# First chunk of a two-layer encoder: modulation rows as stationary operands on TensorE in every quarter, turned x copied by ScalarE, lower parts by VectorE

## The chip, the cores and the metric

The kernel runs on 1 core of one Trainium2 chip. The metric is the device time of one execution in microseconds; lower is better. The engines are named as in the profile: PE is TensorE (PEld its load of stationary operands), DVE is VectorE, ACT is ScalarE, POOL is GpSimd, and SP is the engine whose queue issues the DMAs.

## The reference

Two layers over x (512 tokens by 1024, float32). Only the start of a layer matters here:

```python
cs = silu(c)                                   # (1, 1024)
for l in range(2):
    mod = cs @ w_ada[l] + b_ada[l]             # 3072 columns
    shift, scale, gate = split(mod, 3)
    h = rms_norm(x, norm_g[l]) * (1 + scale) + shift
    proj = h @ w_in[l]                         # 3712 columns
    ...                                        # three kinds of heads, each with a gate
    x = x + gate * (concat(oa, ob, oc) @ w_out[l])
```

So `mod` is a product of one row with a 1024x2048 matrix (shift and scale), needed before the first product of h with `w_in`, and it must be summed over 1024 rows of `w_ada`.

## The kernel before

Every big product is made in float32 precision out of three products of parts: a factor is split into an upper part (the copy to `fp32r`, always by ACT) and a lower part (the difference, by DVE or POOL), and `products` (L331 to L333) multiplies upper by upper, upper by lower and lower by upper. hT and hL are the two parts of the turned h, `whi` and `wlo` (in the first chunk `stq`, `stk` and, for the odd quarters, `stB`, `stC`) those of the weights.

The first chunk multiplies h by 768 columns of `w_in` (for the retention heads). It runs over four quarters q of D (256 columns of h each, so also 256 rows of `w_in`), and in each over four tiles of 128 tokens: `first_chunks`, 16 groups of 12 products into PSUM tiles `acc` (512 columns) and `scw` (256 columns). A quarter can start when its piece of the modulation is there. For that the class `Start` loads eight "rows" of w_ada per quarter (row r holds 128 rows of the matrix, one per partition, by 512 columns, 256 of shift and 256 of scale) and sums them weighted by `cs`:

- rows named in `PE_ROWS[q]` are multiplied on PE, with `cs[:, r]` as stationary operand of one column and the row as 512 moving columns, into one PSUM row `line` (L517); before, this is so for six rows of quarter 0 alone;
- of the others ACT makes the first (`act(self.a, w, AF.Copy, scale=v)`), and DVE adds each of the rest to `ada_acc` (L159 by way of `stt`);
- `close` sums `ada_acc` over the partitions by four products with the 128x128 blocks of `ada_acc` as stationary operand and one column of ones (`over_rows`, L510), and turns `line` into columns by way of an SBUF copy `lsb` and four 1x1 products. The result `ada_ps` is read by DVE into `mod`.

```python
        def over_rows(self, w, v, stop=False):
            ps = self.ps.rearrange("p j k -> p (j k)")
            for i in range(4):
                T.matmul(ps[:, i:i + 1], w[:, i * P:(i + 1) * P], v, start=False, stop=stop and i == 3)
```

Meanwhile x is loaded in four token tiles x0 to x3; `norm_x` squares and sums each on ACT (`junk`), takes the root on DVE and POOL (`rstd`) and scales it in two halves (`xn`, the engine of each by a letter of `X_NORM`); `turn_x` transposes 128x128 blocks on PE into PSUM (`xps`, L1210) and copies them out (`xT`, engines by `X_OUT`). `Start.turn` makes hT (ACT), h (DVE) and hL (engines by `H_SUB`: V is DVE, G is POOL). `Wide.split` makes the weights' parts, with the lower part of one half on POOL and of the other on DVE (L375).

The string `START` gives the order in which these steps are written out; from it a scheduler sets the order of the instructions on each engine, and each engine runs its own in that order. The rows of w_ada go through a pool of five buffers of two rows each (`raw`); SP issues a load only when its buffer is free, in the order of the program.

Of the kernel before, what the change touches and what calls it, by code (L numbers as in the profile page):

```python
# [19 lines left out]
P = 128  # L20
# [34 lines left out]
PE_ROWS = (0, 2, 4, 5, 6, 7), (), (), ()  # L55
# [3 lines left out]
X_NORM, X_OUT, H_SUB, LINE = "AGAGVAVV", "AVVVAVVVAVAVAAAV", "VGGVVGVVGV", "AAAAAAAV"  # L59
# [75 lines left out]
def encoder(ctx, tc, x, c, norm_g, w_ada, b_ada, w_in, w_out, params, consts, out):  # L135
# [222 lines left out]
    class Wide:  # L358
# [10 lines left out]
        def split(self):  # L369
            z = [one.tile([P, 3 + (n != "stC"), S], F32R, name=n) for n in (("stq", "stk"), ("stB", "stC"))[self.q % 2]]  # L370
            self.hi, self.lo = (y.rearrange("p a n -> p (a n)")[:, :1536].rearrange("p (k n) -> p k n", k=2) for y in z)
            for j in range(2):
                c_ = slice(j * 384, j * 384 + 384)
                act(self.hi[:, :, c_], self.raw[j])
                (V if j else G).tensor_tensor(self.lo[:, :, c_], self.raw[j], self.hi[:, :, c_].bitcast(F32), OP.subtract)  # L375
# [107 lines left out]
    ENG = {"V": V, "G": G}  # L483

    def copy(e, o, i):
        V.tensor_copy(o, i) if e == "V" else act(o, i)

    class Start:
# [11 lines left out]
        def open(self):  # L500
            q = self.q
            self.ps = ps = pv_p.tile([P, 2, 2], F32, name="ada_ps", tag="pv")
            self.a = self.line = None
# [8 lines left out]
        def row(self, r):  # L512
            w, v = self.raw[r], cs[:, r:r + 1]
            if r in PE_ROWS[self.q]:
                if self.line is None:
                    self.line = acc_p.tile([P, 512], F32, name="line", tag="acc")
                T.matmul(self.line[0:1], v, w, start=r == PE_ROWS[self.q][0], stop=r == PE_ROWS[self.q][-1])  # L517
# [6 lines left out]
        def close(self):  # L524
            q, ps = self.q, self.ps
            if self.a is not None:
                self.over_rows(self.a, ones[:, 0:1], self.line is None)
            if self.line is not None:
                z = one.tile([P, 512], F32, name="lsb", tag="s9")
                for i in range(2):  # L530
                    copy(LINE[2 * q + i], z[0:1, i * 256:i * 256 + 256], self.line[0:1, i * 256:i * 256 + 256])
                self.over_rows(z[0:1], ones[0:1, 0:1], True)
# [4 lines left out]
        def turn(self, ts):  # L537
# [4 lines left out]
            for k in range(2):  # L542
# [5 lines left out]
                ENG[H_SUB[(2 * q + 2 if q else ts[0]) + k]].tensor_tensor(lo, h[:, :n], hi.bitcast(F32), OP.subtract)  # L548
# [643 lines left out]
    def norm_x(t):  # L1192
# [6 lines left out]
        for j in range(2):  # L1199
# [3 lines left out]
            else:  # L1203
                ENG[X_NORM[2 * t + j]].tensor_scalar(*z, rs, None, OP.mult)

    def turn_x(t, q):
# [4 lines left out]
        for k in range(2):  # L1211
            copy(X_OUT[4 * q + t + k], xT[2 * q + k][:, t * P:(t + 2) * P], ps[:, k].rearrange("p t m -> p (t m)"))
# [82 lines left out]
```

## Time and profile before

| | us |
|---|---|
| median of 3 runs (675.12 to 678.33) | 677.21 |
| the profiled execution, its own time | 676.71 |
| its span, first to last instruction | 674.9 |
| PE busy | 630.2 (93%) |
| DVE busy | 501.0 (74%) |
| ACT busy | 330.4 (49%) |
| POOL busy | 261.4 (39%) |

The span is that of the program's own instructions. Busy time is the union of an engine's instructions; PE's matmuls overlap one another, so of PE the distance from one start to the next tells more than a duration. A float32 product is recorded as two passes. Granted clock is the share of TensorE's full 2.4 GHz, of which the profile knows two levels, 0.50 and 1.00.

### The profile page before, as it was taken

What the parts mean: (1) busy time and instruction counts of PE and PEld (TensorE: products, weight loads), DVE (VectorE), ACT (ScalarE), POOL (GpSimd) and SP (SyncE); (2) the same over time, 40 slices, a digit from 0 to 9 for tenths busy, and PEclk for the clock granted to TensorE, in tenths of its full rate; (3) what the DMA queues carried; (4) which work ended last, traced back from release to release, by engine and by line L of the source; (5) the groups of instructions that cost most, each with busy time, mean ns of one, the idle gap of its engine ahead of it and who ended that gap; (6) DMA issues with size and microseconds to landing.
All of it is one profiled execution on the core that took longest, in us unless ns stands there. A gap on an engine that the chain in (4) does not pass through costs nothing.

```text
span 674.9 us, 10503 instructions
## 1 busy us (share of the span) xinstructions
PE 630.2 (93%) x3487; PEld 516.0 (76%) x3487; DVE 501.0 (74%) x1157; ACT 330.4 (49%) x722; POOL 261.4 (39%) x252
## 2 busy tenths in 40 slices
PE   6889998999999996999998999989999999989997
PEld 2778787977887784677776998887778887767786
DVE  1998697589988988897769154768997888576443
ACT  5534352447655674554423243434757476656410
POOL 3427363666343520211457252767052613121200
PEclk9789998999999999899999999999999999999999
DMA  9796133344555556575643122235454625423211
GB/s 316 250 335 159 57 94 97 105 120 120 148 127 173 144 165 170 166 243 181 216 166 119 32 83 75 64 84 155 114 156 119 193 85 161 116 64 133 93 63 63
DMA packets 87134, 93.20 MB, mean 138 GB/s; under 512 B 7044, under 2 KB 68004, under 8 KB 87080
## 3 DMA queue, kind: packets, MB, share of 16 engines
q1 hardware_dynamic: 87080, 92.53, 45.6%
q8 instruction: 28, 0.46, 0.3%
q14 instruction: 26, 0.21, 0.1%
HBM read 72.58 MB, written 4.19 MB: 114 GB/s over the span
## 4 chain that ended last, share of the span: by engine, by line
PE 41%; DVE 8%; POOL 4%; issue 2%; ACT 2%; DMA 0%; POOLq 0%; ACTq 0%; DVEq 0%; SPq 0%
PE acc L333 8%; PE acc L332 8%; PE acc L331 8%; PE tr L554 5%; PE pv L703 3%; PE acc L327 1%; PE acc L329 1%; PE acc L328 1%; DVE wlo L302 1%; PE sc L726 1%; PE sc L787 1%; DVE ada_acc L159 1%; PE sc L788 1%; DVE pt L693 1%; PE ada_ps L464 1%
## 5 line engine op out<-in xcount | busy, mean ns | idle before, releaser
L331 PE MATMUL acc<-whi,hT 128*128 128x384 f32 (+1 forms) x424 | 155.4, 366 | 1.5 <-ACT vc L156 1.0
L333 PE MATMUL acc<-whi,hL 128*128 128x384 f32 (+1 forms) x424 | 153.2, 361 | 0.0
L332 PE MATMUL acc<-wlo,hT 128*128 128x384 f32 (+1 forms) x424 | 152.7, 360 | 0.0
L302 POOL TENSOR_TENSOR wlo<-raw,whi 128x768 fp32r<-128x768 f32 (+1 forms) x26 | 55.1, 2119 | 126.4 <-ACT whi L156 119.2
L156 ACT ACTIVATE whi<-raw 128x768 fp32r<-128x768 f32 (+1 forms) x75 | 69.6, 929 | 52.9 <-PE acc L333 41.6
L331 PEld LDWEIGHTS acc<-whi,hT 128*128 128x128 f32 x424 | 80.2, 189 | 8.5 <-ACT vc L156 1.4
L302 DVE TENSOR_TENSOR wlo<-raw,whi 128x384 fp32r<-128x384 f32 (+1 forms) x98 | 64.1, 683 | 28.6 <-ACT whi L156 28.3
L333 PEld LDWEIGHTS acc<-whi,hL 128*128 128x128 f32 x424 | 80.1, 189 | 6.2
L332 PEld LDWEIGHTS acc<-wlo,hT 128*128 128x128 f32 x424 | 80.2, 189 | 5.7
L159 DVE SCALAR_TENSOR_TENSOR ada_acc<-raw,cs,ada_acc 128x512 f32<-128x512 f32 x86 | 72.3, 845 | 5.3 <-DMA raw<-in_w_ada_dram 2.7
L199 POOL TENSOR_TENSOR qkss<-qkss,nhalf 128x4 f32<-128x4 f32 (+1 forms) x40 | 54.1, 1352 | 49.2 <-DVE qkss L569 48.2
L156 ACT ACTIVATE e<-sc,mx 128x512 f32<-128x512 f32 x64 | 43.9, 688 | 37.7 <-DVE mx L728 23.3
L728 DVE TENSOR_REDUCE mx<-sc 128x1 f32<-128x512 f32 x64 | 43.1, 684 | 9.9 <-PE sc L726 9.6
L156 ACT ACTIVATE sb<-sb,mx 128x512 f32<-128x512 f32 x48 | 34.5, 719 | 29.1 <-DVE mx L792 27.9
L703 PE MATMUL pv<-pt,v 128*64 128x256 f32 x320 | 38.9, 385 | 3.8 <-DVE pt L693 3.8
L693 DVE COPY pt<-tr 128x512 f32<-128x512 f32 x40 | 27.4, 686 | 15.7 <-PE tr L554 15.6
L156 ACT ACTIVATE pt<-tr 128x512 f32<-128x512 f32 x40 | 23.8, 596 | 29.1 <-PE tr L554 29.0
L554 PE MATMUL tr<-cst,sb 128*128 128x128 f32 x192 | 30.9, 284 | 6.4 <-DVE nat L159 2.4
L703 PEld LDWEIGHTS pv<-pt,v 128*64 128x64 f32 x320 | 21.2, 136 | 19.1 <-DVE pt L693 8.4
L554 PEld LDWEIGHTS tr<-cst,sb 128*128 128x128 f32 x192 | 22.0, 142 | 17.2 <-ACT pt L156 8.1
L792 DVE CUSTOM_DVE_ANT_0 sb<-sc,cst 128x512 f32<-128x512 f32 x48 | 32.0, 682 | 3.8 <-PE sc L788 3.0
L624 POOL TENSOR_TENSOR qkn<-qkraw,qkss 128x256 f32<-128x256 f32 x40 | 28.9, 722 | 5.0 <-DVE ga L620 2.0
(298 smaller groups left out, 1433.1 us busy)
## 6 DMA issues: line engine op xcount, KB each, us to landing
raw<-in_w_ada_dram SPq DMA_DIRECT2D x64, 256.0 KB, 4.0
raw<-in_w_in_dram SPq DMA_DIRECT2D x48, 192.0 KB, 2.7
raw<-in_w_in_dram SPq DMA_DIRECT2D x24, 384.0 KB, 3.5
raw<-in_w_in_dram SPq DMA_DIRECT2D x32, 256.0 KB, 3.5
raw<-in_w_ada_dram SPq DMA_DIRECT2D x16, 512.0 KB, 4.6
raw<-in_w_out_dram SPq DMA_DIRECT2D x32, 256.0 KB, 3.2
x<-in_x_dram SPq DMA_DIRECT2D x8, 512.0 KB, 3.4
stB<-nat SPq DMA_DIRECT2D x32, 128.0 KB, 2.4
```

The source lines that it names most:

```text
L156: A.activation(o, i, f, **kw)
L159: V.scalar_tensor_tensor(o, a, s, b, op0, op1)
L199: G.tensor_tensor(o, i, nhalf[:, :n], OP.pow)
L302: (G if pool else V).tensor_tensor(l2[:, z], r2[:, z], h2[:, z].bitcast(F32), OP.subtract)
L331: T.matmul(ps, ah, hi[i], start=s_, stop=False)
L332: T.matmul(ps, ah, lo[i], start=False, stop=False)
L333: T.matmul(ps, al, hi[i], start=False, stop=e_)
L554: T.transpose(ps[:, i, :], b, ident)
L693: V.tensor_copy(pt, ps)
L703: T.matmul(self.pv[h * 64:h * 64 + 64, i * 256:i * 256 + 256], self.u.v[:, k, h * 64:h * 64 + 64], self.pt[h][:, k], start=k == 0, stop=k ...
L728: V.tensor_reduce(mx, ps, AX.X, OP.max, negate=True)
L792: V.tensor_tensor_reduce(sb, ps, cst[:, m0:m0 + S], 1.0, 3e38, OP.add, OP.min, mx)
```

## The change

It touches the first chunk alone. `PE_ROWS` names rows in every quarter: six of quarter 0 as before, three of quarter 1, two each of quarters 2 and 3. A row on PE is no longer a one-column stationary operand with 512 moving columns: its four 128x128 blocks are the stationary operands, with `cs[:, r]` as one moving column, straight into `ada_ps`; `line`, `lsb` and the 1x1 products go. ACT makes all copies of turned x. DVE makes all lower parts of the first chunk (hL and both halves of the weights') and all of `xn` that ACT doesn't. POOL keeps the roots and the clearing of tiles.

```diff
--- before.py
+++ after.py
@@ -52,11 +52,11 @@
 X_BACK = 2
 
 
-PE_ROWS = (0, 2, 4, 5, 6, 7), (), (), ()
+PE_ROWS = (0, 2, 4, 5, 6, 7), (2, 4, 6), (4, 6), (4, 6)
 
 
 START = "xxbiaaataxfxwrthsttthttrvrrt"
-X_NORM, X_OUT, H_SUB, LINE = "AGAGVAVV", "AVVVAVVVAVAVAAAV", "VGGVVGVVGV", "AAAAAAAV"
+X_NORM = "AVAVVAVV"
 
 _CONST = {}
 
@@ -372,7 +372,7 @@
             for j in range(2):
                 c_ = slice(j * 384, j * 384 + 384)
                 act(self.hi[:, :, c_], self.raw[j])
-                (V if j else G).tensor_tensor(self.lo[:, :, c_], self.raw[j], self.hi[:, :, c_].bitcast(F32), OP.subtract)
+                V.tensor_tensor(self.lo[:, :, c_], self.raw[j], self.hi[:, :, c_].bitcast(F32), OP.subtract)
 
     def first_chunks(ret):
 
@@ -480,11 +480,6 @@
     def mod_steps(l, q):
         return ada_steps(l, [(q * 256, 256), (D + q * 256, 256)], lambda ps: mod_use(q, ps, mod_gain(l, q)))
 
-    ENG = {"V": V, "G": G}
-
-    def copy(e, o, i):
-        V.tensor_copy(o, i) if e == "V" else act(o, i)
-
     class Start:
 
 
@@ -500,7 +495,7 @@
         def open(self):
             q = self.q
             self.ps = ps = pv_p.tile([P, 2, 2], F32, name="ada_ps", tag="pv")
-            self.a = self.line = None
+            self.a = None
 
             T.matmul(ps, bias[:2 * KD, 0], ident[:2 * KD].rearrange("p (a j k) -> p a j k", j=2, k=KD)[:, 0, :, 2 * q:2 * q + 2], start=True, stop=False)
 
@@ -512,9 +507,7 @@
         def row(self, r):
             w, v = self.raw[r], cs[:, r:r + 1]
             if r in PE_ROWS[self.q]:
-                if self.line is None:
-                    self.line = acc_p.tile([P, 512], F32, name="line", tag="acc")
-                T.matmul(self.line[0:1], v, w, start=r == PE_ROWS[self.q][0], stop=r == PE_ROWS[self.q][-1])
+                self.over_rows(w, v)
             elif self.a is None:
                 self.a = two.tile([P, 512], F32, name="ada_acc")
                 act(self.a, w, AF.Copy, scale=v)
@@ -523,13 +516,7 @@
 
         def close(self):
             q, ps = self.q, self.ps
-            if self.a is not None:
-                self.over_rows(self.a, ones[:, 0:1], self.line is None)
-            if self.line is not None:
-                z = one.tile([P, 512], F32, name="lsb", tag="s9")
-                for i in range(2):
-                    copy(LINE[2 * q + i], z[0:1, i * 256:i * 256 + 256], self.line[0:1, i * 256:i * 256 + 256])
-                self.over_rows(z[0:1], ones[0:1, 0:1], True)
+            self.over_rows(self.a, ones[:, 0:1], True)
             m = self.m = one.tile([P, 2, 2], F32, name=f"mod0{q}")
             stt(m[:, 1], ps[:, 1], 1.0, ngt[:, 2 * q:2 * q + 2], OP.add, OP.mult)
             V.tensor_copy(m[:, 0], ps[:, 0])
@@ -545,7 +532,7 @@
                 act(hi, x_, AF.Identity, bias=shift, scale=scale)
                 h = ep.tile([P, S], F32, name="h", tag="e")
                 V.tensor_scalar(h[:, :n], x_, scale, shift, OP.mult, OP.add)
-                ENG[H_SUB[(2 * q + 2 if q else ts[0]) + k]].tensor_tensor(lo, h[:, :n], hi.bitcast(F32), OP.subtract)
+                V.tensor_tensor(lo, h[:, :n], hi.bitcast(F32), OP.subtract)
 
 
     def tr4(blocks):
@@ -1201,7 +1188,7 @@
             if X_NORM[2 * t + j] == "A":
                 act(*z, AF.Copy, scale=rs)
             else:
-                ENG[X_NORM[2 * t + j]].tensor_scalar(*z, rs, None, OP.mult)
+                V.tensor_scalar(*z, rs, None, OP.mult)
 
     def turn_x(t, q):
         ps = acc_p.tile([P, 2, 2, P], F32, name="xps", tag="acc")
@@ -1209,7 +1196,7 @@
             for i in range(2):
                 T.transpose(ps[:, k, i], xn[t + i][q // 2][:, (q % 2 * 2 + k) * P:(q % 2 * 2 + k + 1) * P], ident)
         for k in range(2):
-            copy(X_OUT[4 * q + t + k], xT[2 * q + k][:, t * P:(t + 2) * P], ps[:, k].rearrange("p t m -> p (t m)"))
+            act(xT[2 * q + k][:, t * P:(t + 2) * P], ps[:, k].rearrange("p t m -> p (t m)"))
 
     def start_x(t):
         dma(x_sb[t], x[0, tok_(t)])
```

How the order moves on PE at the start, from the first small product of the modulation on. Before (L517 is a row of w_ada as moving operand, L510 the closing sums, L1210 a transpose of x, `scw<-stq` the first products of the chunk):

```order
L505 MATMUL ada_ps<-cst,bias 128x4
L1227 MATMUL gps<-cst,bias 128x8
L517 MATMUL line<-raw,cs 1x512 x4
L1210 MATMUL xps<-cst,xn 128x128 x4
L517 MATMUL line<-raw,cs 1x512 x2
L510 MATMUL ada_ps<-ones,ada_acc 128x1 x4
L510 MATMUL ada_ps<-ones,lsb 128x1 x4
L1210 MATMUL xps<-cst,xn 128x128 x3
L505 MATMUL ada_ps<-cst,bias 128x4
L1210 MATMUL xps<-cst,xn 128x128 x17
L331 MATMUL scw<-stq,hT 128x256 x2
L332 MATMUL scw<-stk,hT 128x256
```

And now (L505 is a row of w_ada, or `ada_acc`, as stationary operand; L1197 a transpose):

```order
L505 MATMUL ada_ps<-cs,raw 128x1 x4
L1197 MATMUL xps<-cst,xn 128x128
L505 MATMUL ada_ps<-cs,raw 128x1 x16
L505 MATMUL ada_ps<-ones,ada_acc 128x1 x4
L500 MATMUL ada_ps<-cst,bias 128x4
L1197 MATMUL xps<-cst,xn 128x128 x16
L331 MATMUL scw<-stq,hT 128x256
L332 MATMUL scw<-stk,hT 128x256
L1197 MATMUL xps<-cst,xn 128x128 x8
L505 MATMUL ada_ps<-cs,raw 128x1 x4
L1197 MATMUL xps<-cst,xn 128x128 x4
L331 MATMUL acc<-stq,hT 128x512
```

Six rows of four products each stand where six 512-column products stood, and a row of quarter 1 and twelve transposes now stand between the first product with `stk` and the first into `acc` (before: eight transposes).

On ACT at the same place, before (`junk` is the squaring of a tile of x; `x_95` and `x_96` are x2 and x3; hT needs the modulation of quarter 0):

```order
L156 ACTIVATE ada_acc<-raw,cs 128x512
L156 ACTIVATE xT_126<-xps 128x256
L156 ACTIVATE junk,rstd<-x_95 128x1024
L156 ACTIVATE lsb<-line 1x256 x2
L156 ACTIVATE xn<-x_95,rstd 128x512
L156 ACTIVATE junk,rstd<-x_96 128x1024
L156 ACTIVATE hT<-xT_126,mod_212 128x256
L156 ACTIVATE hT<-xT_127,mod_212 128x256
L156 ACTIVATE stq<-whi 128x2x384
```

And now:

```order
L156 ACTIVATE ada_acc<-raw,cs 128x512
L156 ACTIVATE xT_126<-xps 128x256
L156 ACTIVATE xT_127<-xps 128x256
L156 ACTIVATE hT<-xT_126,mod_222 128x256
L156 ACTIVATE hT<-xT_127,mod_222 128x256
L156 ACTIVATE junk,rstd<-x_95 128x1024
L156 ACTIVATE xn<-x_95,rstd 128x512
L156 ACTIVATE junk,rstd<-x_96 128x1024
L156 ACTIVATE stq<-whi 128x2x384
```

The two hT of the first token tiles have moved ahead of the squares of x2 and x3.

On DVE from the modulation of quarter 0 on, now (L375 is a lower part of the weights, L1191 the scaling of x, L534 h, L535 hL):

```order
L159 SCALAR_TENSOR_TENSOR mod_222<-ada_ps,ngt 128x2
L522 COPY mod_222<-ada_ps 128x2
L534 TENSOR_SCALAR h<-xT_126,mod_222 128x256
L534 TENSOR_SCALAR h<-xT_127,mod_222 128x256
L535 TENSOR_TENSOR hL<-h,hT 128x256 x2
L556 TENSOR_SCALAR rstd<-rstd 128x1
L1191 TENSOR_SCALAR xn<-x_95,rstd 128x512
L556 TENSOR_SCALAR rstd<-rstd 128x1
L1191 TENSOR_SCALAR xn<-x_96,rstd 128x512 x2
L375 TENSOR_TENSOR stk<-whi,stq 128x2x384
L375 TENSOR_TENSOR stk<-wlo,stq 128x2x384
```

Both lower parts of the first weights stand on DVE behind the scaling of x3; before, one of them was on POOL.

## Rows read from the trace of the kernel before

**Rows 1.** The page, busy time of PE and DVE (us, share of the span, instructions) and PE's busy tenths in 40 slices of the span.
```profile
PE 630.2 (93%) x3487; PEld 516.0 (76%) x3487; DVE 501.0 (74%) x1157; ACT 330.4 (49%) x722; POOL 261.4 (39%) x252
...
PE   6889998999999996999998999989999999989997
```

**Rows 2.** Busy time of each engine by stretches of 20 us: stretch, its length, busy us (instructions) of each engine, granted clock of PE, share of the DMA engines, GB/s.
```profile
20.00:40.00 20.00, 16.93 (x88) 14.04 (x87) 19.35 (x32) 8.04 (x16) 7.91 (x7) 0.88 0.79 249
40.00:60.00 20.00, 18.22 (x102) 15.84 (x101) 17.91 (x29) 6.17 (x9) 8.06 (x9) 0.91 1.02 304
60.00:80.00 20.00, 19.02 (x96) 15.40 (x95) 14.34 (x56) 8.24 (x20) 9.81 (x19) 1.00 0.23 67
```

**Rows 3.** PE in order of time, from the first small product to the first 512-column product of the chunk: start us, us, what, out<-in, shapes, count of passes, and in brackets the idle time before it and what ended it.
```profile
6.45 0.55 PE L505 MATMUL ada_ps<-cst,bias 16*128 16x4 f32 x2 [4.10 <-DMA cst<-in_consts_dram]
6.87 0.25 PE L1227 MATMUL gps<-cst,bias 8*128 8x8 f32 x1
7.05 5.57 PE L517 MATMUL line<-raw,cs 128*1 128x512 f32 x8
...
13.13 1.88 PE L517 MATMUL line<-raw,cs 128*1 128x512 f32 x4
14.94 1.05 PE L510 MATMUL ada_ps<-ones,ada_acc 128*128 128x1 f32 x8
...
17.69 3.13 PE L1210 MATMUL xps<-cst,xn 128*128 128x128 f32 x13
21.23 0.65 PE L1210 MATMUL xps<-cst,xn 128*128 128x128 f32 x4 [0.42 <-ACT xT L156]
21.64 0.66 PE L331 MATMUL scw<-stq,hT 128*128 128x256 f32 x2
24.44 0.38 PE L332 MATMUL scw<-stk,hT 128*128 128x256 f32 x1 [2.15 <-DVE stk L375]
...
25.05 1.91 PE L1210 MATMUL xps<-cst,xn 128*128 128x128 f32 x8
26.61 0.77 PE L331 MATMUL acc<-stq,hT 128*128 128x512 f32 x1
```

**Rows 4.** The 512-column passes of the modulation on PE, grouped: busy us, mean ns of one; first in the stretch 7 to 9.6 us, then in 11 to 15 us.
```profile
L517 PE MATMUL line<-raw,cs 128*1 128x512 f32 x4 | 3.6, 1049 | 0.0
...
L517 PE MATMUL line<-raw,cs 128*1 128x512 f32 x8 | 4.1, 632 | 0.0
```

**Rows 5.** Stretches around the changes of the granted clock; columns as in rows 2; the clock is the third number from the end.
```profile
17.90:21.20 3.30, 2.92 (x13) 2.15 (x11) 2.64 (x8) 3.30 (x7) 2.06 (x4) 0.50 1.08 361
21.30:24.60 3.30, 1.15 (x7) 0.84 (x8) 3.30 (x4) 2.05 (x5) 1.67 (x1) 1.00 1.10 352
24.70:28.10 3.40, 3.40 (x15) 3.11 (x15) 3.35 (x10) 1.76 (x5) 1.82 (x4) 0.50 0.84 265
...
45.20:48.50 3.30, 3.30 (x13) 2.82 (x12) 3.16 (x5) 1.52 (x2) 0.25 (x1) 0.50 1.06 389
```

**Rows 6.** ACT in order of time around the first hT.
```profile
13.98 1.06 ACT L156 ACTIVATE junk<-x 128x1024 f32<-128x1024 f32 x1 [0.36 <-DMA x<-in_x_dram]
...
16.01 0.72 ACT L156 ACTIVATE xn<-x,rstd 128x512 f32<-128x512 f32 x1 [0.32 <-POOL rstd L199]
16.64 1.04 ACT L156 ACTIVATE junk<-x 128x1024 f32<-128x1024 f32 x1
...
17.68 1.07 ACT L156 ACTIVATE hT<-xT,mod 128x256 fp32r<-128x256 f32 x2
```

**Rows 7.** DVE in order of time, from the scaling of a half tile of x to the last `stk`.
```profile
16.01 0.48 DVE L1204 TENSOR_SCALAR xn<-x,rstd 128x512 f32<-128x512 f32 x1 [0.69 <-POOL rstd L199]
17.01 0.16 DVE L159 SCALAR_TENSOR_TENSOR mod<-ada_ps,ngt 128x2 f32<-128x2 f32 x1 [0.51 <-PE ada_ps L510]
...
23.44 0.94 DVE L375 TENSOR_TENSOR stk<-wlo,stq 128x768 fp32r<-128x768 f32 x1
```

**Rows 8.** PE in order of time around its closing sums and at the end of the chunk (`acc<-whi` belongs to the next unit).
```profile
34.84 0.95 PE L510 MATMUL ada_ps<-ones,ada_acc 128*128 128x1 f32 x8
35.65 0.36 PE L331 MATMUL scw<-stq,hT 128*128 128x256 f32 x1
...
37.01 0.50 PE L331 MATMUL acc<-stB,hT 128*128 128x512 f32 x1 [0.45 <-ACT hT L156]
...
43.81 1.05 PE L510 MATMUL ada_ps<-ones,ada_acc 128*128 128x1 f32 x8 [1.78 <-DVE ada_acc L159]
44.72 0.48 PE L332 MATMUL acc<-stC,hT 128*128 128x512 f32 x1
...
68.52 0.39 PE L331 MATMUL acc<-whi,hT 128*128 128x512 f32 x1
...
72.46 0.51 PE L331 MATMUL acc<-whi,hT 128*128 128x512 f32 x1 [0.98 <-ACT vc L156]
```

**Rows 9.** Groups of DVE and POOL by form: busy us, mean ns of one, idle before. The first three are DVE in 20 to 58 us, the last is POOL in 18 to 60 us.
```profile
L159 DVE SCALAR_TENSOR_TENSOR ada_acc<-raw,cs,ada_acc 128x512 f32<-128x512 f32 x21 | 19.5, 940 | 0.4
...
L375 DVE TENSOR_TENSOR stC<-wlo,stB 128x768 fp32r<-128x768 f32 x2 | 3.5, 1773 | 0.0
...
L375 DVE TENSOR_TENSOR stk<-wlo,stq 128x768 fp32r<-128x768 f32 x2 | 1.9, 947 | 0.0
...
L375 POOL TENSOR_TENSOR stC<-whi,stB 128x768 fp32r<-128x768 f32 x2 | 4.4, 2181 | 0.0
```

## The prediction

> **What bounds the kernel now.** I read the page first: TensorE (PE) is busy for 93% of the span and VectorE (DVE) for 74%, and only the first slices of the PE row stand well under nine tenths [rows 1]. So a change to the first chunk can only matter through the moment at which PE gets through that chunk; behind it PE is the bound, and a shift there is carried to the end nearly one to one. The table of windows then shows that in 20 to 40 us DVE is the busier engine (19.35 against 16.93 of 20 us) and that from 60 us on PE is [rows 2]. PE reaches the last product of the first chunk just before 68.52, where the next unit's products begin [rows 8].
>
> Next I looked for what PE waits for inside the chunk. Behind 21.6 us it waits four times: 2.15 us for `stk` (the lower parts of the weights, made on DVE), 0.45 for hT, 1.78 for the DVE sum of the modulation, and 0.98 just after the chunk [rows 3, 8]. The windows around two of these waits show the second cost: after each, the granted clock is 0.50 for some 3.4 us (24.70 to 28.10, 45.20 to 48.50) [rows 5], the lower of TensorE's two levels, 1.2 against 2.4 GHz, and each such stretch of full work loses 1.7 us. These are the prizes that the change could win: 2.15 + 1.78 of waiting and 2 x 1.7 of clock, 7.3 us.
>
> **The price of a row on PE.** Each row of the modulation that moves to PE becomes four products with a 128x128 stationary operand and one moving column, and the profile counts two records (passes) for each, so eight passes. The trace of before has this very form: the closing sum (`ones,ada_acc`, 128x1, x8) takes from 34.84 to 35.65 and from 43.81 to 44.72 until the next product starts [rows 8], 0.86 us on average at a granted clock of 1.00, or 0.1 us a pass. Nothing hides it: PE works in order and is the busy engine.
>
> At 0.50 no row has one-column passes with a full stationary operand. The nearest are the small starting products with 4 and 8 columns, 0.2 us apart (6.45, 6.87, 7.05), and the eight transposes from 25.05 to 26.61, 0.195 each, which took 0.1 each at 21.23 to 21.64 [rows 3]. So the bounds are 0.1 and 0.21 a pass. I take 0.21, since both near rows double with the clock.
>
> **The clock of the first quarter** is the term that decides. Before, PE starts with six rows as 512-column passes: their mean is 1049 ns early and 632 ns in 11 to 15 us [rows 4]. The profile shows 1.00 there, but the durations tell that PE starts at the lower level and goes up after some 4 us of these passes. From 14.94 on PE runs one-column passes, 16 of them, and then transposes, without a wait, and behind them the granted clock is 0.50 for 17.90 to 21.20 [rows 3, 5]. The change takes out the 512-column passes and leaves one-column passes and four transposes. I expect PE to stay at 0.50 through this quarter.
>
> Step by step from 7.05, where the first row is there: 48 passes for six rows and 8 for the closing sum, 56 x 0.21 = 11.8; four transposes 0.8; a little latency 0.3: the modulation is read at 19.95, against 17.01 before [rows 7]. What goes: 12 passes `line` (7.05 to 14.94, with four transposes among them) [rows 3], two ACT copies of a one-partition row and eight of those 16 one-column passes (the 1x1 products). At 0.1 a pass from 11 us on, the same sum gives 15.9.
>
> **What queues behind it on ScalarE (ACT).** The order of ACT now has both hT of the first two token tiles ahead of the squares of x2 (`junk`); before, x2 went at 13.98 and hT at 17.68 [rows 6]. hT waits for the modulation, and the squares of x2 and x3, their scaling on DVE and both `stk` wait behind it. From 19.95: hT 0.2 + 1.07 gives 21.2; squares to scaled x2 take 2.03 (13.98 to 16.01) [rows 6], then 0.65 until ACT starts the squares of x3 at 23.85; again 2.03 gives 25.9; two scalings on DVE at 0.48 [rows 7] give 26.85; two `stk` at 0.95 [rows 9], now both on DVE, 28.75. Before, the last `stk` began at 23.44 and PE went on at 24.44 [rows 3, 7]. That is **+4.3**.
>
> From there to the first 512-column product (26.61 before, 2.17 later) PE has 12 transposes and one row instead of 8 transposes: 20 passes and a product, 2.2 us at 1.00 and 4.2 at 0.50. PE has just waited, as before 24.44, and there the transposes ran at 0.50; I take 4.2: **+2.0**.
>
> **The rest of the chunk.** DVE loses 7 rows of 0.94 [rows 9] and the copies of turned x, and gains four lower parts of 0.95 and half of the hL. It also loses its neighbour: the same subtraction took 947 ns and 1773 ns on DVE, the longer ones while GpSimd ran its own of 2181 [rows 9]. So I see DVE in time for every closing sum from here on: the waits of 1.78 and 0.45 go (-2.2), and with the first the stretch at 0.50 behind it (-1.7) [rows 5, 8]. PE pays six rows at 0.86 (+5.2) and three small products of 0.1 that now come later (+0.3). Together **+1.6**. ACT's added copies cost nothing here: it is busy for 8 and 6 of 20 us [rows 2]. The loads keep their order; a later buffer only delays loads that lie well ahead of their use once PE is late itself. The wait of 0.98 behind the chunk comes from small DVE work for ACT, which is now early: **-1.0**.
>
> Sum: 4.3 + 2.0 + 1.6 - 1.0 = +6.9. The profiled execution took 676.7 us in all (674.9 its span), so **683.6 us**; the median shown is 0.5 above that execution, so this is 0.9% above the median.
>
> **Rivals.**
> Full clock early. If PE goes to 2.4 GHz by 11 us in spite of its one-column passes, the modulation comes at 15.9, every step behind it 4.05 earlier: `stk` at 24.7 (+0.3), transposes at full clock (0.0), the rest +1.6 - 1.0: +0.9, 677.6. For it speaks that PE is never idle there; against it the 0.50 from 17.90 on [rows 5], also without idling.
>
> DVE relief wins, the case on the other side. If the modulation comes by 15.5 (all rows had landed by 13.13, where the last two were used [rows 3], plus 24 passes of 0.1) and `stk` is there before PE asks for it at 21.9, both waits and both stretches at 0.50 go: -7.3, -1.5 for the earlier modulation, -1.0 behind the chunk, against 7 rows +6.0: -3.8, 672.9. Its point is whether `stk` comes by 21.9; the chain on ACT and DVE of 8.8 us behind the modulation speaks against it.
>
> Transposes do not lift the clock. In this kernel the granted clock rose at 21.3 after a stretch in which PE ran transposes only [rows 3, 5]. If they did not count, PE would also run its first 3.4 us of products at 0.50: +1.7, 685.3. The Trainium skill, "TensorE: Matmul & The Clock Gate", section "Part 4: PE-mode transpose", says so: a transpose does not count as busy for the clock, and the full rate does not engage for it. By that rule this rival would be the forecast; the trace does not agree with it (0.50 in 17.90 to 21.20 with transposes, 1.00 behind).
>
> **How the numbers follow.** Forecast 0.60, full clock early 0.22, DVE relief 0.10, transposes 0.08. Under 0.5% (3.4 us) a measurement of this kernel can't tell a change from none. Slower: most of the first case and the last, 0.64. Same: most of the second and the near edge of the first, 0.25. Faster: 0.11. The range takes in the second case with 2 us below it for DVE relief in part, and above the forecast 4 us (the last rival, and loads that come late): 675.5 to 687.5. The forecast's own range is 680 to 687.
>
> **What would show it.** Right: the granted clock or the spacing of one-column passes tells 0.2 us a pass in 7 to 19 us; the modulation is read near 20; the squares of x2 start on ACT after 21; the first product of the chunk with `stk` near 28.7; then no wait of PE on DVE over 0.5 us, and the first product of the next unit near 75 to 76 instead of 68.5. Wrong: passes of 0.1 us before 15, `stk` at 25 or earlier, or new waits of PE at a row that has not landed.

## The result

The changed kernel takes 684.1 us (median of 5 runs, 681.28 to 684.69) beside 677.21 of before (675.0 to 679.07): ratio 1.0097, interval 1.0072 to 1.0121, so it is slower by 0.7 to 1.2%. The forecast was 683.6. The first profiled execution of it took 681.28 (span 679.5), the fastest of its five; a second one, from other runs of the same kernel (684.27 in the median, ratio 1.0104, 1.0067 to 1.0141), took 684.25 (span 682.5) and is told of under the last experiment. Where the text says "after", it means the first.

### The profile page after: what moved, and what is told of

Read it like the earlier page. It is cut to its first block, busy times and chain, and to the rows that moved or that the text cites. A ratio compares the mean times of both kernels' runs of the same rounds, so it can differ in the third digit from the quotient of the medians.

```text
span 679.5 us, 10652 instructions
## 1 busy us (share of the span) xinstructions
PE 637.4 (94%) x3571; PEld 531.9 (78%) x3571; DVE 491.2 (72%) x1151; ACT 332.8 (49%) x729; POOL 247.0 (36%) x242
## 4 chain that ended last, share of the span: by engine, by line
PE 39%; DVE 9%; POOL 4%; issue 2%; ACT 2%; DMA 2%; SPq 0%; POOLq 0%; DVEq 0%; ACTq 0%
PE acc L333 8%; PE acc L332 8%; PE acc L331 8%; PE tr L541 5%; PE pv L690 3%; DVE wlo L302 1%; PE acc L329 1%; PE acc L327 1%; PE acc L328 1%; DVE ada_acc L159 1%; PE sc L713 1%; DMA raw<-in_w_in_dram 1%; PE sc L774 1%; DMA raw<-in_w_ada_dram 1%; PE sc L775 1%
## 5 line engine op out<-in xcount | busy, mean ns | idle before, releaser
L159 DVE SCALAR_TENSOR_TENSOR ada_acc<-raw,cs,ada_acc 128x512 f32<-128x512 f32 x79 | 63.1, 799 | 5.8 <-DMA raw<-in_w_ada_dram 4.4
L541 PEld LDWEIGHTS tr<-cst,sb 128*128 128x128 f32 x192 | 21.9, 142 | 17.3 <-ACT pt L156 8.1
L611 POOL TENSOR_TENSOR qkn<-qkraw,qkss 128x256 f32<-128x256 f32 x40 | 28.9, 722 | 4.7 <-ACT th L156 1.7
```

The costliest lines, as they stand in the source:

```text
L159: V.scalar_tensor_tensor(o, a, s, b, op0, op1)
L541: T.transpose(ps[:, i, :], b, ident)
L611: (V if (E_SCALE_A if n == DK_A else E_SCALE_B) % 2 else G).tensor_tensor(self.qn[t], self.raw[t].rearrange("p (g n) -> p g n", n=n), self ...
```

## The profile after

The page: PE is busier than in [rows 1], and its first slices still stand below nine tenths.

```profile
PE 637.4 (94%) x3571; PEld 531.9 (78%) x3571; DVE 491.2 (72%) x1151; ACT 332.8 (49%) x729; POOL 247.0 (36%) x242
...
PE   6799998999999997899998999989999999989997
```

Busy time by stretches of 20 us, columns as in [rows 2]: DVE has fallen from 19.35 and 17.91 to 10.93 and 13.86, PE is now the busier engine from 20 us on, and the granted clock, 0.88 and 0.91 before, is shown as 1.00.

```profile
20.00:40.00 20.00, 16.10 (x93) 14.47 (x93) 10.93 (x23) 13.06 (x29) 2.66 (x5) 1.00 0.64 193
40.00:60.00 20.00, 20.00 (x133) 17.97 (x133) 13.86 (x24) 6.82 (x9) 0.53 (x1) 1.00 0.94 292
```

PE in order of time, columns as in [rows 3], from the first product to the next unit's.

```profile
6.92 0.56 PE L500 MATMUL ada_ps<-cst,bias 16*128 16x4 f32 x2 [4.57 <-DMA cst<-in_consts_dram]
7.34 0.25 PE L1214 MATMUL gps<-cst,bias 8*128 8x8 f32 x1
7.52 1.87 PE L505 MATMUL ada_ps<-cs,raw 128*128 128x1 f32 x8
...
11.73 6.83 PE L505 MATMUL ada_ps<-cs,raw 128*128 128x1 f32 x32
18.42 1.84 PE L505 MATMUL ada_ps<-ones,ada_acc 128*128 128x1 f32 x8
...
24.14 2.40 PE L1197 MATMUL xps<-cst,xn 128*128 128x128 f32 x10 [2.91 <-DVE xn L1191]
...
28.88 0.58 PE L332 MATMUL scw<-stk,hT 128*128 128x256 f32 x1 [0.37 <-DVE stk L375]
29.25 1.61 PE L1197 MATMUL xps<-cst,xn 128*128 128x128 f32 x8
30.70 0.95 PE L505 MATMUL ada_ps<-cs,raw 128*128 128x1 f32 x8
31.51 0.63 PE L1197 MATMUL xps<-cst,xn 128*128 128x128 f32 x4
31.90 0.47 PE L331 MATMUL acc<-stq,hT 128*128 128x512 f32 x1
...
37.30 0.95 PE L505 MATMUL ada_ps<-cs,raw 128*128 128x1 f32 x8
38.11 0.48 PE L333 MATMUL acc<-stq,hL 128*128 128x512 f32 x1
38.43 0.39 PE L331 MATMUL acc<-stq,hT 128*128 128x512 f32 x1
...
74.40 0.39 PE L331 MATMUL acc<-whi,hT 128*128 128x512 f32 x1
```

The 32 passes from 11.73 to 18.42 take 0.21 us each, the 8 from 30.70 to 31.51 take 0.1. The records know no change of the clock ahead of a rise at 30.42, and the column shows 1.00 until there; the spacing of the passes tells that PE ran at the lower level up to that moment. A row at the full clock costs 0.81 until the next product and 0.09 in it (38.11 to 38.43, where such products otherwise stand 0.23 apart): 0.90.

What waits behind the modulation, on ACT and on DVE (compare [rows 6, 7]): the modulation is read at 20.30, hT goes ahead of the squares of x2 (`junk`, 21.62), and the last `stk` begins at 27.87.

```profile
20.63 1.09 ACT L156 ACTIVATE hT<-xT,mod 128x256 fp32r<-128x256 f32 x2 [7.99 <-DVE mod L522]
21.62 1.04 ACT L156 ACTIVATE junk<-x 128x1024 f32<-128x1024 f32 x1
```

```profile
20.30 0.16 DVE L159 SCALAR_TENSOR_TENSOR mod<-ada_ps,ngt 128x2 f32<-128x2 f32 x1 [9.76 <-PE ada_ps L505]
...
27.87 0.95 DVE L375 TENSOR_TENSOR stk<-wlo,stq 128x768 fp32r<-128x768 f32 x1
```

The groups of DVE in 20 to 58 us, columns as in [rows 9]: an addition of a row takes 750 ns instead of 940, a lower part of the odd quarters' weights 954 instead of 1773 (the mean of one that took 2.60 us and one that took 0.95, see under before_plus_rows).

```profile
L159 DVE SCALAR_TENSOR_TENSOR ada_acc<-raw,cs,ada_acc 128x512 f32<-128x512 f32 x14 | 10.5, 750 | 0.6 <-ACT ada_acc L156 0.4
...
L375 DVE TENSOR_TENSOR stC<-wlo,stB 128x768 fp32r<-128x768 f32 x1 | 1.0, 954 | 0.0
```

## The experiments

Three theories went in. A: the loss is the late start, since the six rows of quarter 0 as stationary operands run at 0.50 and what queues behind the modulation waits; the seven rows of the other quarters cost 0.9 each. B: the loss is those seven rows, and the late start is absorbed. C: DVE, with all lower parts, is late. Their results, beside a kernel before of 676.2 to 677.7 in the same runs ("us" is the ratio's part above 1 times 677.2; the ratio takes in all runs, so it can differ from that of the two medians, most in q0_as_line):

| kernel | median us | ratio, interval | us |
|---|---|---|---|
| the change | 684.10 | 1.0097 (1.0072 to 1.0121) | +6.6 |
| q0_as_line | 677.11 | 0.9969 (0.9946 to 0.9992) | -2.1 |
| q0_rows_alone | 677.55 | 0.9988 (0.9973 to 1.0003) | -0.8 |
| line_alone | 670.85 | 0.9887 (0.9870 to 0.9904) | -7.7 |
| before_plus_rows | 680.63 | 1.0037 (1.0021 to 1.0053) | +2.5 |
| keep_clock | 686.50 | 1.0131 (1.0095 to 1.0168) | +8.9 |
| squares_first | 681.72 | 1.0060 (1.0038 to 1.0083) | +4.1 |
| lower_parts_alone | 673.35 | 0.9944 (0.9931 to 0.9958) | -3.8 |
| line_warm | 671.41 | 0.9915 (0.9900 to 0.9931) | -5.8 |
| three_rows | 675.47 | 0.9988 (0.9971 to 1.0006) | -0.8 |
| three_rows_q0_only | 671.22 | 0.9928 (0.9904 to 0.9952) | -4.9 |
| no_rows | 672.18 | 0.9931 (0.9909 to 0.9953) | -4.7 |
| change_again | 684.27 | 1.0104 (1.0067 to 1.0141) | +7.0 |

### Undoing one part, and both

**q0_as_line**: the change with the rows of quarter 0 in their old form.

```diff
-                self.over_rows(w, v)
+                if self.q == 0:
+                    if self.line is None:
+                        self.line = acc_p.tile([P, 512], F32, name="line", tag="acc")
+                    T.matmul(self.line[0:1], v, w, start=r == PE_ROWS[0][0], stop=r == PE_ROWS[0][-1])
+                else:
+                    self.over_rows(w, v)
```

(and in `close` the sum over `lsb`, as before, copied by ACT.) With the old form the scheduler also put ACT's old order back: in the trace the squares of x2 and x3 (15.13 and 17.75) stand ahead of hT (18.79). So this edit undoes two things, here and in line_alone; squares_first, below, takes up the order alone.

> The changed kernel with its six rows of quarter 0 back in the old form (one-column stationary operand, 512 moving columns, line and lsb); everything else as changed. Theory A, the late start: the changed kernel lost its time because PE stayed at 0.50 through quarter 0, so the modulation came at 20.3 and, behind hT on ACT, the first product into acc at 31.9. Here the 512-column passes lift the clock by about 11 us, the modulation is read near 17, the first product into acc starts at 25 to 26.5, 5.5 to 7 us earlier, and the time is 677 to 679. Theory B, the rows: the seven rows that PE got in quarters 1 to 3 (7 x 0.86 = 6.0 us) are the loss and the start is absorbed later: 683 to 684. Theory C, DVE: lower parts moved from GpSimd make DVE late: 683 to 684, with waits of PE on DVE.

**q0_rows_alone**: the change without rows on PE in the other quarters.

```diff
-PE_ROWS = (0, 2, 4, 5, 6, 7), (2, 4, 6), (4, 6), (4, 6)
+PE_ROWS = (0, 2, 4, 5, 6, 7), (), (), ()
```

> The changed kernel with rows on PE in quarter 0 alone (as stationary operands); DVE and ACT sum the rows of quarters 1 to 3 as before the change. Theory A: the start stays late (first product into acc at about 31), and 6.0 us of PE work go; DVE, which cannot begin these sums before 28.7, may let PE wait for up to 2 us at the first closing sum: 678 to 681. Theory B: the loss is gone, 676 to 678. Theory C: PE waits on DVE for the 6 us that it saves, 683 to 685.

**line_alone**: both edits at once, so that of the change only ACT's copies and DVE's lower parts are left.

> As the kernel with quarter 0 in the old form, and quarters 1 to 3 have no row on PE either: of the change only ACT's copies of turned x and DVE's lower parts are left. Theory A: start as in the old form, and 6.0 us less of PE work; DVE has 7 rows more at 0.75 and no GpSimd beside it, so PE's waits on closing sums stay under 2 us in all: 671 to 674. Theory B: 677 to 678, the same as before the change. Theory C: PE waits on DVE for over 3 us, 678 to 684.

**before_plus_rows**: before, with the seven rows of quarters 1 to 3 as stationary operands.

```diff
-PE_ROWS = (0, 2, 4, 5, 6, 7), (), (), ()
+PE_ROWS = (0, 2, 4, 5, 6, 7), (2, 4, 6), (4, 6), (4, 6)
...
-            if r in PE_ROWS[self.q]:
+            if r in PE_ROWS[self.q] and self.q:
+                self.over_rows(w, v)
+            elif r in PE_ROWS[self.q]:
```

> The kernel before with one part of the change: rows 2, 4, 6 of quarter 1 and 4, 6 of quarters 2 and 3 go to PE as stationary operands; quarter 0, GpSimd's share and the copies stay as before. Theory A: 7 x 0.86 = 6.0 us more on PE, against the wait of 1.78 us on the closing sum, 0.45 us for hT and a stretch at 0.50 (1.7 us) that go: +1 to +2.5, 678 to 680. Theory B: +6, 683. Theory C: DVE is relieved of 7 rows, so faster than before, 673 to 675.

All four lie in A's ranges or within 0.7 us of them. But the 677.55 of q0_rows_alone lies in B's range (676 to 678) and just under A's, so that run by itself does not tell the two apart. B falls by q0_as_line and line_alone, where it expected 683 to 684 and 677 to 678, C by q0_rows_alone and before_plus_rows. By the ratios the change is made up of three parts: ACT's copies and DVE's lower parts take 7.7 us off; the stationary form of the six rows of quarter 0 costs 8.7 with the seven rows (1.0097 against 0.9969) and 6.8 without (0.9988 against 0.9887); the seven rows cost 7.4 and 5.6. Those pairs agree within what the intervals allow, so each of the two costs is known to some 2 us only. line_alone beats both kernels.

The profiles divide it less evenly. The first product of the next unit, at 68.52 before and at 74.40 after, comes at 70.94 in q0_as_line, 69.32 in q0_rows_alone and 62.50 in line_alone. Up to there the stationary form costs 3.5 with the seven rows and 6.8 without, the rows 5.1 and 8.4. The odd one is q0_as_line. Its modulation was read at 18.36 and its first product into `acc` came at 27.02, both later than A expected (near 17, 25 to 26.5), and PE ran at the lower clock for ten us there:

```profile
20.10:30.30 10.20, 9.58 (x39) 8.60 (x39) 8.42 (x16) 9.06 (x22) 1.58 (x3) 0.50 0.96 309
```

Its twelve runs form two groups, 4 us apart: five of 671.8 to 674.8 at a mean granted clock of 0.987 to 0.992, and seven of 677.0 to 678.4 at 0.984. The profile is of the second group; what the start looks like in the first is not shown.

On before the seven rows cost 2.5 only, though PE pays the same 0.9 each: they take away the wait of 1.78 for DVE's sum, the 0.45 for hT and the stretch at 0.50 behind the first of these [rows 5, 8], of which its trace has none. And there DVE's instructions are no quicker for its relief: beside GpSimd, which makes the other half, its groups in 20 to 58 us were

```profile
L159 DVE SCALAR_TENSOR_TENSOR ada_acc<-raw,cs,ada_acc 128x512 f32<-128x512 f32 x14 | 14.6, 1043 | 0.6 <-ACT ada_acc L156 0.3
L375 DVE TENSOR_TENSOR stC<-wlo,stB 128x768 fp32r<-128x768 f32 x2 | 6.8, 3398 | 0.3 <-ACT stB L156 0.3
```

while in line_alone, with all of it on DVE, they were

```profile
L159 DVE SCALAR_TENSOR_TENSOR ada_acc<-raw,cs,ada_acc 128x512 f32<-128x512 f32 x21 | 15.6, 748 | 0.4
...
L375 DVE TENSOR_TENSOR stC<-wlo,stB 128x768 fp32r<-128x768 f32 x2 | 1.9, 950 | 0.0
```

The means mix two kinds of instruction. Of the two `stC` that DVE made before, one began while GpSimd made a subtraction of its own; the other ran for the most part beside clearings of tiles on GpSimd:

```profile
28.50 2.60 DVE L375 TENSOR_TENSOR stC<-wlo,stB 128x768 fp32r<-128x768 f32 x1
...
54.42 0.95 DVE L375 TENSOR_TENSOR stC<-wlo,stB 128x768 fp32r<-128x768 f32 x1
```

```profile
27.99 2.30 POOL L375 TENSOR_TENSOR stC<-whi,stB 128x768 fp32r<-128x768 f32 x1
```

In before_plus_rows both ran beside GpSimd's subtractions, and took 2.49 and 4.31 us. So a subtraction on DVE takes 0.95 us, or that and about as long as GpSimd's work beside it.

**lower_parts_alone** splits the gain: before, with DVE's lower parts and its halves of `xn`, but the copies of turned x as before.

```diff
-X_NORM, X_OUT, H_SUB, LINE = "AGAGVAVV", "AVVVAVVVAVAVAAAV", "VGGVVGVVGV", "AAAAAAAV"
+X_NORM, X_OUT, H_SUB, LINE = "AVAVVAVV", "AVVVAVVVAVAVAAAV", "VVVVVVVVVV", "AAAAAAAV"
...
-                (V if j else G).tensor_tensor(self.lo[:, :, c_], self.raw[j], self.hi[:, :, c_].bitcast(F32), OP.subtract)
+                V.tensor_tensor(self.lo[:, :, c_], self.raw[j], self.hi[:, :, c_].bitcast(F32), OP.subtract)
```

> The kernel before with one part of the change alone: VectorE makes all lower parts and the halves of xn that ScalarE doesn't; the copies of turned x stay split between ScalarE and VectorE, the rows of the modulation stay as before. ScalarE's copies and these lower parts together took 6.8 us off before. Theory N (GpSimd as neighbour slows VectorE): the lower parts alone carry most of that, 671 to 673. Rival R (VectorE is only relieved by giving its copies to ScalarE): lower parts alone add work to VectorE, 677 to 681.

It gains 3.8 us, and its median of 673.35 lies just above N's range. Rival R is out, and by the ratios N carries half of the 7.7, not most; in its profile the next unit begins at 67.00, which is 1.5 of the 6.0 us that line_alone has gained by there. With ten instructions more (1167) DVE was busy for 497.8 us instead of 501.0, since each takes less: in 20 to 58 us ada_acc 750 ns, stC 998. The Trainium skill, "GPSIMD Engine Reference", section "1. Specifications", says that GpSimd shares its way into the SBUF with VectorE and contends with VectorE's instructions that have two inputs there; the trace agrees for the subtractions, which have two (0.95 us, or 2.49 to 4.31 beside GpSimd's). The rest of the gain comes with ACT's copies.

### The clock and the queues

**keep_clock**: the change, with products of zeros (bf16, 512 columns) among the rows of quarter 0.

```diff
+    def work(n):
+        w, y = zeros[0]
+        for _ in range(n):
+            tc.keep_in_program_order(T.matmul(w, y[:, :P], y, start=False, stop=False))
...
+        work(10)
...
                 self.over_rows(w, v)
+                if self.q == 0:
+                    work(2)
```

> The kernel after, with products of zeros (bf16, 512 columns, added to scw) put in among the rows of quarter 0: ten ahead of the first row, two behind each of the six. If the late start comes from the lower clock in quarter 0 (theory A), the passes of the rows take 0.1 us instead of 0.21, the modulation is read near 15.5 to 16.5 instead of 20.3, and the total is near 680 (4 less than the change). Rival: 0.21 us is the price of a 128x128 stationary operand whatever the clock; then the zeros only add work: 684 to 686.

The total, 686.5, missed both, by 0.5 above the rival's range. But the trace answers the question that the kernel was for. PE in order of time:

```profile
8.00 1.02 PE L514 MATMUL ada_ps<-cs,raw 128*128 128x1 f32 x8
8.88 0.59 PE L382 MATMUL scw<-zero 128*128 128x512 bf16 x2
...
12.26 1.71 PE L514 MATMUL ada_ps<-cs,raw 128*128 128x1 f32 x8
13.82 1.01 PE L382 MATMUL scw<-zero 128*128 128x512 bf16 x2
14.63 1.71 PE L514 MATMUL ada_ps<-cs,raw 128*128 128x1 f32 x8
```

and its clock by stretches:

```profile
7.06:10.47 3.41, 2.69 (x21) 2.19 (x21) 1.21 (x5) 3.14 (x6) 1.00 (x2) 1.00 1.05 335
10.47:20.90 10.43, 10.19 (x45) 8.97 (x47) 0.66 (x1) 0.55 (x2) 0.00 (x0) 0.50 1.02 359
```

The same row takes 0.88 us until the next product at 1.00 and 1.56 at 0.50: the 0.21 is the clock, not the operand, so the rival is out. And the zeros ahead did bring the full clock, but at 10.47, behind 3.41 us in which PE was busy for 2.69, it fell again, and it stayed down though PE was busy for 10.19 of the next 10.43 us, with 512-column products after each row. At 0.50 the zeros cost 0.4 each, and the modulation came at 23.49. So the run doesn't show what the change would take with a quarter 0 at the full clock; these products did not keep it there.

**squares_first**: the change, with the first hT on ACT behind the squares of x3.

```diff
+    def turn_behind(ts):
+        with tc.issue_after(squares[3].ins):
+            mod.turn(ts)
...
-             "h": [(mod.turn, (0, 1)), (mod.turn, (2, 3))]}
+             "h": [(turn_behind, (0, 1)), (mod.turn, (2, 3))]}
```

> The kernel after, with the order on ScalarE alone changed: the first hT goes behind the squares of x3. If what queues behind hT on ScalarE carries the late modulation on to the weights' lower parts (theory A), the modulation is still read near 20.3, the squares of x2 go near 14 and the first product of 512 columns comes near 28.4 instead of 31.9: total near 680.5. Rival (the late modulation itself is the loss, in whatever order ScalarE works): 683.5 to 684.5.

The squares of x2 did go early, at 13.69, and nothing came of it: DVE's queue holds the root of x2 behind the reading of the modulation, and ACT then waited for it. ACT and DVE in order of time:

```profile
13.69 1.06 ACT L156 ACTIVATE junk<-x 128x1024 f32<-128x1024 f32 x1 [1.47 <-DMA x<-in_x_dram]
...
21.68 0.72 ACT L156 ACTIVATE xn<-x,rstd 128x512 f32<-128x512 f32 x1 [6.84 <-POOL rstd L199]
```

```profile
19.89 0.16 DVE L159 SCALAR_TENSOR_TENSOR mod<-ada_ps,ngt 128x2 f32<-128x2 f32 x1 [9.68 <-PE ada_ps L505]
...
20.88 0.15 DVE L556 TENSOR_SCALAR rstd<-rstd 128x1 f32<-128x1 f32 x1
```

The first 512-column product came at 31.24, not 28.4, at a clock that rose at 34.67 only, and the next unit's at 75.18, not earlier than 74.40. The median, 681.72, lies between the two expectations and 2.5 us under the change by the ratios, which the profile of this run does not bear out; what that is stays open. ACT's order alone is not what carries the delay.

**three_rows**: the change, with three rows of quarter 0 on PE and the others on DVE, which idles there (9.76 us ahead of 20.30).

```diff
-PE_ROWS = (0, 2, 4, 5, 6, 7), (2, 4, 6), (4, 6), (4, 6)
+PE_ROWS = (0, 2, 4), (2, 4, 6), (4, 6), (4, 6)
```

> The kernel after with three rows of quarter 0 on TensorE instead of six (0, 2, 4; VectorE adds 3, 5, 6, 7 to ada_acc); the seven rows of the other quarters stay as in the change. Theory A (the number of stationary passes at the lower clock makes the modulation late, and that costs 7 us): 24 passes go, VectorE has the last rows at 13.1 + 2 x 0.75 and the closing sum takes 1.7, so the modulation is read near 16.5 instead of 20.3 and the total is 676.5 to 678. Rival (the start is lost by the order on ScalarE and by idle TensorE, not by these passes): 681 to 684.

This is the clearest support for A: the form is the same, the passes of quarter 0 take the same 0.21 us, 24 of the 56 are gone, and 7.4 us come back (1.0097 to 0.9988). The median, 675.47, is even 1 us under A's range, and the next unit begins at 67.75 instead of 74.40. PE and DVE in order of time:

```profile
11.76 1.71 PE L505 MATMUL ada_ps<-cs,raw 128*128 128x1 f32 x8
13.49 1.87 PE L505 MATMUL ada_ps<-ones,ada_acc 128*128 128x1 f32 x8
```

```profile
11.11 2.33 DVE L159 SCALAR_TENSOR_TENSOR ada_acc<-raw,cs,ada_acc 128x512 f32<-128x512 f32 x3 [0.53 <-DMA raw<-in_w_ada_dram]
15.40 0.16 DVE L159 SCALAR_TENSOR_TENSOR mod<-ada_ps,ngt 128x2 f32<-128x2 f32 x1 [1.96 <-PE ada_ps L505]
```

DVE was done at 13.4, sooner than expected, and the modulation was read 4.9 us earlier than in the change. The clock rose at 22.15, ahead of the first product with `stk` (24.69); in the change it rose at 30.42, behind that product (28.88). How much of the 7.4 is the earlier rise and how much the earlier modulation, the run doesn't separate.

**three_rows_q0_only** and **no_rows**: the same with `PE_ROWS = (0, 2, 4), (), (), ()`, and with four empty tuples.

> The same, and no rows on TensorE in the other quarters. If the costs of start and rows add up, 6.3 to 6.5 less than three_rows: 670 to 671.5, as line_alone (670.85), without its row of sums and copy. Rival: VectorE, which now adds 11 rows more in all, is late with its closing sums or lower parts: 672 to 675.

> The same with no row on TensorE in any quarter: VectorE adds all rows but the first. It keeps pace with the landing of the rows (two rows of 0.75 for each pair, the last pair at 13.1), so the modulation is read near 16.6 and the total is 670 to 672. Rival: VectorE also has the halves of xn at the start and falls behind: modulation at 18 or later, 672 to 675; or TensorE, idle, starts its transposes at the lower clock and stays there longer, 672 to 673.

671.22 is in the first one's range, but the seven rows were worth 4.1 us here, not 6.3: without them PE waits 1.6 us for hL from DVE, which they would have covered. In no_rows the modulation came at 17.20, between the two expectations (PE waited 5.2 us for DVE's sum), and the time, 672.18, is where both ranges meet. Neither takes less time than line_alone.

**line_warm**: line_alone, with ten products of zeros ahead of the first row (`work(10)`, as in keep_clock).

> ScalarE's copies and VectorE's lower parts on the kernel before (line_alone, 670.85), with ten products of zeros on TensorE ahead of its first row, so that it may be at the full clock when the first row comes. If the clock at the start is on the path: the first four rows' passes at 632 ns instead of 1049, the modulation read 1 to 1.5 us earlier and 1 to 2 off the total, 669 to 670. Rival: the rows' landing (13.1) or ScalarE sets the modulation anyway: 670.5 to 671.5.

The modulation came at 16.20 instead of 16.97, but the clock fell at 16.89 and stayed down until 23.72, against 17.61 to 21.02 in line_alone; the next unit began at 63.68 against 62.50. Its ratio is above that of line_alone, and its median of 671.41 is in the rival's range: the warm start bought nothing.

### The change once more

**change_again**: the changed kernel as it is, for a second profile.

> The changed kernel once more, unchanged, for a second profile. Its first profiled run was the fastest of five (681.28 beside 683.8 to 684.7), and there the granted clock rose at 30.42, before the last transposes ahead of the first 512-column product. If that moment differs from run to run and makes the scatter, a run of 683 to 685 shows the rise some 3.4 us later, near 33.8, the first 512-column product at 32.5 to 33 instead of 31.90 and the next unit at 76 or later instead of 74.40. Rival: the rise is at 30.4 whatever the time, and the slower runs lose theirs behind the chunk: the next unit at 74.4 again.

For this run the rival holds. The rise was again before 31 us, the first 512-column product came at 31.62 and the next unit at 74.13; the 3 us by which this run is longer arose behind the chunk. To place them, I took the starts of the 1156 products with `whi` into `acc` behind the chunk, in the same order in all three traces, and their distance to before:

| product (its time before) | after, us later | change_again, us later |
|---|---|---|
| first of the next unit (68.52) | 5.88 | 5.61 |
| 72.46 | 4.74 | 4.47 |
| 89.18 | 3.16 | 2.89 |
| 188.51 | 3.34 | 3.33 |
| 274.37 | 3.39 | 4.40 |
| 446.24 | 5.47 | 7.20 |
| 596.13 | 4.65 | 7.57 |

So nearly half of what the chunk loses is given back within 21 us: 1.1 at the place of the wait for `vc` [rows 8] and more behind it, where before also shows

```profile
PE tr L554 <- DVE qfb L905: 1.0, 1, 1.0
```

(PE's waits in 68 to 98 us: us, times, longest), and neither run of the change has a wait there. What comes on top, far behind the change, stands at stretches of lower clock. In change_again (columns as in [rows 5]):

```profile
446.50:453.30 6.80, 5.80 (x25) 5.83 (x26) 4.81 (x9) 1.42 (x4) 2.87 (x4) 0.50 0.41 117
...
600.10:603.50 3.40, 3.23 (x10) 2.60 (x11) 3.00 (x9) 1.42 (x3) 0.53 (x2) 0.50 0.00 0
...
275.90:279.20 3.30, 3.30 (x11) 2.58 (x11) 3.23 (x10) 0.68 (x2) 1.06 (x1) 0.50 0.62 225
```

after has only the first half of the first of these,

```profile
446.90:450.20 3.30, 3.23 (x13) 3.26 (x14) 1.59 (x5) 0.47 (x1) 1.76 (x3) 0.50 0.58 182
```

and before has neither of the first two:

```profile
442.00:446.00 4.00, 2.98 (x24) 3.01 (x25) 2.22 (x6) 0.97 (x3) 1.90 (x3) 1.00 0.47 147
590.00:600.00 10.00, 8.00 (x48) 5.31 (x49) 6.75 (x18) 4.42 (x11) 3.49 (x3) 1.00 0.27 80
```

Around the third before has one of its own (270.5 to 273.8). In all, behind the chunk and ahead of the last 3 us of the span, before has two stretches at 0.50, after three, and change_again five, one of which is twice as long as the others (446.5 to 453.3). In these distances the one at 275.9 costs 1.1 us, the one at 600.1 costs 1.2, the long one at 446.5 costs 2.7 and the single one of after 1.5; of those at 446 some 0.7 comes back by 462, where before waits 0.6 for `v` from ACT and the change does not. They make the 3 us between these two runs.

Two more things stand in the record. Such stretches are no mark of the change: three_rows_q0_only is at 0.50 in 436.9 to 440.1 as well, and line_warm in 436.8 to 440.0 and 587.0 to 590.2. The mean granted clock of before goes from 0.977 to 0.989 over its 17 runs beside three_rows, so it too spends more time at the lower clock in some runs than in others. And they are not all of the scatter: the runs of the change that took 683.83 and 684.10 have a mean granted clock of 0.992 and 0.991, as the first profile with its 681.28 has (0.992; change_again 0.985). What makes those 2.5 to 2.8 us longer stays open. The mean counts the time ahead of the first record as full clock, so a later rise at the start would not show in it.

## Why the prediction was right, and where it was not

The total was right (+6.9 forecast, +6.6 and +7.0 by the ratios), and so was the first half of its working. Behind that, errors offset one another, and that the total was met so closely is in part luck.

**Quarter 0** was right. PE stayed at 0.50 with 0.21 us a pass, and the modulation was read at 20.30 (19.95 forecast; PE started 0.47 later, when its constants landed). keep_clock shows that 0.21 is the clock, three_rows that the count of passes makes the delay. "Full clock early" is out.

**What queues behind it** was right in size: 28.88 for the product with `stk`, 28.75 forecast, +4.44 instead of +4.3. That ACT's order is the reason was too simple: squares_first freed ACT, and DVE's own queue, with the roots behind the modulation, held the chain as long (the last `stk` began at 27.93 there, at 27.87 in the change).

**Transposes and one row at 0.50** was mis-sized: +2.0 forecast, +0.85 measured (3.02 us from 28.88 to 31.90, 2.17 before). I had taken the whole stretch at the lower clock from the place before where PE had just waited 2.15 us; here it waited 0.37 and had run transposes and two products since 24.14, and the clock rose at 30.42.

**The rest of the chunk**: +1.6 forecast, +0.6 measured (42.50 us from 31.90 to 74.40, 41.91 before). No wait of PE is left in it, and none of its clock is lost, as forecast; rows cost 0.90 instead of 0.86. Left out of the sum was the end of the low stretch that before still has behind its first product (26.61 to 28.10, so 0.75 us), which goes too; some 0.5 us more of the difference is not placed. The next unit began at 74.40 and 74.13, not at "75 to 76".

**Behind the chunk**: -1.0 forecast for the wait of 0.98, -1.1 measured there, but about -2.7 by 89 us; further on +1.5 in the first profile (the stretch of low clock at 446.9 and a wait of 0.4 for `wlo`, less the 0.7 that comes back) and +4.7 in the second (stretches of low clock), where the forecast had nothing. So the parts were 7.9 - 1.0 in the forecast, 5.9 - 2.7 + 1.5 in the first profile and 5.6 - 2.7 + 4.7 in the second, which is near the median. The forecast of 683.6 came within 0.5 of the median of 684.1 because a term of +4.7 that was not in the sum made up for parts that the sum had too high.

**The rivals.** "DVE relief wins" named the right prize: 7.3 us of waits and low clock, and line_alone, which takes it without paying for rows and a late modulation, gains 7.7, though a wait of 1.6 for hL and one stretch of low clock are left in its start. In the change the price was higher than the prize: the product with `stk` came at 28.9, far behind 21.9. "Transposes do not lift the clock" falls by line_alone, whose clock was 0.50 in 17.7 to 21.0 and 1.00 behind, with transposes alone on PE from 17.65 to 21.61:

```profile
17.65 3.93 PE L1207 MATMUL xps<-cst,xn 128*128 128x128 f32 x17
21.61 0.39 PE L331 MATMUL scw<-stq,hT 128*128 128x256 f32 x1
```

```profile
17.70:21.00 3.30, 3.19 (x15) 2.56 (x15) 2.64 (x7) 3.05 (x7) 0.92 (x2) 0.50 1.08 362
21.10:24.50 3.40, 3.21 (x19) 2.25 (x19) 3.37 (x7) 3.40 (x11) 1.08 (x3) 1.00 1.10 351
```

The Trainium skill, "TensorE: Matmul & The Clock Gate", section "Part 4: PE-mode transpose", says otherwise: the full clock does not engage for transposes. Here the measurement decides, for these transposes of float32.

## What to carry to other kernels

Cost each part of a change by itself: here a part worth 7.7 us was hidden behind two that cost some 7 each by the ratios, and a version with that part alone beat both kernels. Before small products take over a sum at the start, count their passes at the clock that they will run at, and look on every engine's queue for what stands behind their result. A forecast that meets the median has not yet been shown right: follow one landmark after another through both traces, and take a second profile of the same kernel before a difference far from the edit is put down to it.

## What was not expected of the hardware

- PE can be busy without a gap and yet stay at the lower clock: behind 13 us of one-column passes and four transposes (6.92 to 19.90, busy for all of it) passes still took 0.21 us, and in keep_clock it stayed at 0.50 for 10.43 us in which PE was busy for 10.19.
- The clock column shows 1.00 ahead of the first record of a change, even where passes take twice their time; spacing tells the level there.
- GpSimd beside DVE costs more than its share of the work saves: the same subtraction on DVE took 0.95 us alone and 2.49 to 4.31 beside GpSimd's own, and giving GpSimd's part of the first chunk to DVE took 3.8 us off the kernel.
- Stretches of low clock hundreds of microseconds behind an edit differ between two runs of one kernel, and made 3 us of the 684 between two profiles of the change.
